# Keeping the split parts of shared weights in DRAM, and a third buffer for the gate operands

## The chip, the core and the metric

The kernel runs on one core of one Trainium2 chip. TensorE multiplies, VectorE, ScalarE (ACT) and GpSimd (POOL) do the elementwise work, SyncE (SP) issues most transfers; ACT and POOL issue some. Each engine runs its own instructions in order. The metric is the device time of one execution in microseconds (us). Three runs of the kernel before gave 3194.96, 3195.38 and 3200.4 us, a median of 3195.38.

## The reference

One encoder block over 1024 tokens with a width of 1024, in float32:

```python
xn = rmsnorm(h, attn_norm_w[l])
proj = xn @ w_in                     # q | k | v | conv B | conv C | conv x | gate a | gate b
y_attn = (rmsnorm(attn, subln_w) * (1 - lambda_init)) @ w_pa     # differential attention
y_conv = (bg * short_conv(cg * xc, conv_w)) @ w_pb
h = h + (sigmoid(ga) * y_attn + sigmoid(gb) * y_conv) @ w_o
hn = rmsnorm(h, ffn_norm_w[l])
sc = einsum('chpd,hpnd->chpn', (hn @ w_query), sub_keys)          # 8 heads x 2 x 128 keys
# 16 best of the pair sums per head -> eidx (of 128*128 experts), g = softmax(top)
out = einsum('chk,chkd->cd', g * gelu(einsum('chkd,cd->chk', expert_u[eidx], hn)), expert_v[eidx])
return rmsnorm(h + out, final_norm_w)
```

## The kernel before

**Two parts of each operand.** TensorE takes a float32 operand here as two parts: a rounded high part `wh` and the rest `wl`, and a product is three matmuls (high by high, high by low, low by high, `THREE` in `gemm`). A weight comes in units of 128 x 2048 numbers, 1.05 MB. `unit` (L207) loads one into a raw tile `wr` on SP, `put` (L183) makes `wh` by a cast on ACT and `wl` by a subtraction on VectorE, or on POOL where `cfg["lo"]` says so. The parts go into a ring of two buffers (`wring`, in some stages a second one, `wloc`). The raw tile has one buffer in most stages, two in the first scores.

**Two groups of tokens.** Group B is the first 640 tokens (`GROUPS`, five tiles of 128), group A the last 384 (three tiles). After q, k and v for all tokens, `mixer` runs for group B: `conv` (six units), `gates` for one gate (four), `gated` (two), attention with the other gate's `gates` between its steps (four), and `gated` again (two). `mix` adds the output projection (four units, `units_k` two at a time). `scores` multiplies by the query weights (eight units) and the keys; group B has two calls, for two tiles and for three. Then group A goes through `mixer`, `mix` and `scores` with the same weights, loaded and split again. So 30 units are used by both groups, and the eight query units three times.

**Selection and gate weights.** `select_gen` (VectorE mostly) takes the 16 best experts per head and token, in two halves per tile; each half ends in two reductions `e`. `weights_gen` (L682) turns the choice of group B's tiles into a dense table of gate weights: per step of four tokens VectorE compares (`ms`, L714), POOL and ACT make the operands `o1` (L718) and `o2` (L720), and one step later `finish` multiplies them on TensorE (`pw`, L695) and copies the product into `wbuf` (L696). Every 32 tokens `wbuf` is stored to `w_d` on ACT's queue (L726). `ms`, `o1` and `o2` have two buffers (`WFB`). These generators are advanced by `tick` along the foreground matmuls, and a scheduler sets the final order on each engine.

**The dense stage.** Afterwards group B's tokens go through all 128 rows of experts: `expert_in` (products `z`, Gelu `pr`, times the gate weights `wt` loaded from `w_d`, L920, split into `ph`) and `expert_out` (products `pout` and `held`). Beside it group A's chosen experts are gathered one by one (`gather_gen`).

**Queues.** SP issues in order: a transfer that waits for its tile holds up those behind it. The gate stores and the scores' stores are on ACT's queue, the gathers and q, k loads on POOL's.

Of the kernel before, what the change touches and what calls it, by code (L numbers as in the profile page):

```python
# [10 lines left out]
F32 = mybir.dt.float32  # L11
# [9 lines left out]
P = 128  # L21
# [30 lines left out]
WQ = 4  # L52
WFB = 2
GATHER = 2.0
# [11 lines left out]
def block_kernel(ctx, tc, x, wqkv, wcols, wpr, wo, wq, skT, uv, uT, an_w, fn_w, fin_w, sub_w,  # L66
# [7 lines left out]
    def pool(name, bufs=1, stack=None, **kw):  # L74
        return (stack or left).enter_context(tc.tile_pool(name=name, bufs=bufs, **kw))
# [10 lines left out]
    dram = pool("dram", space=bass.MemoryType.DRAM)  # L86
# [96 lines left out]
    def put(op, sl, src, lo=V):  # L183
        A.copy(out=op[0][sl], in_=src)  # L184
        lo.tensor_sub(op[1][sl], src, op[0][sl].bitcast(F32))  # L185
# [20 lines left out]

    def unit(wp, src, c):  # L207
        t = cfg["raw"].tile([P, 2048], F32, name="wr", tag="wr")
        SP.dma_start(out=t, in_=src)
        op = operand(wp, [P, 2048], "w")  # L210
        put(op, slice(None), t, cfg["lo"])
        return tuple(t.rearrange("p (k c) -> p k c", c=c) for t in op)

    def units_k(wp, src, n):
        u = [unit(wp, src[n, i], 512) for i in range(2)]
        return [tuple(t[:, k % 4, :] for t in u[k // 4]) for k in range(KD)]
# [244 lines left out]
    def conv(g, n, wring, wloc, xT, uTc):  # L461
        with ExitStack() as st:
            wk = pool("convw", 2, stack=st)
            for ct in range(CT):
                if ct % 2 == 0:
                    wc, wx, wb = (unit(w, wcols[2 * j + ct // 2], 256) for w, j in ((wring, 1), (wring, 2), (wloc, 0)))
                    ys = []
# [34 lines left out]
    def gates(n, wring, xT, j, dst):  # L502
        for dt in range(KD):
            if dt % 2 == 0:
                wg = unit(wring, wcols[6 + 4 * j + dt // 2], 256)
            for c0, cn in halves(n):
                pg = ps['g'].tile([P, cn], F32, name="pg", tag="g")
                gemm(pg, kts(wg, slice((dt % 2) * P, (dt % 2 + 1) * P)), kts(xT, slice(c0, c0 + cn)))
                A.activation(dst[:, dt, c0:c0 + cn], pg, AF.Tanh, scale=0.5)
                yield  # L510

    def gated(n, wring, j, src, g, done):
        for dt in range(KD):
            if dt % 4 == 0:
                wp = unit(wring, wpr[j, dt // 4], 512)
            for c0, cn in halves(n):
                ns = slice(c0, c0 + cn)
                py = ps['g'].tile([P, cn], F32, name="py", tag="g")
                gemm(py, kts(wp, slice((dt % 4) * P, (dt % 4 + 1) * P)), kts(src, ns))
                V.scalar_tensor_tensor(g[:, dt, ns], g[:, dt, ns], 1.0, py, op0=ALU.add, op1=ALU.mult)  # L520
                if done:
                    done((slice(None), dt, ns))

    def mix(tt0, nt, c0, keep_hn, rings, mT, hnT, outer=None):
        with ExitStack() as st:
# [10 lines left out]
            for j in range(2):  # L536
                w = units_k(rings[j], wo, j)
                for i in range(nt):
# [17 lines left out]
    def scores(tt0, nt, c0, rings, hnT, sk, first=None):  # L556
        with ExitStack() as st:
# [14 lines left out]
            for hp in range(2 * PH):  # L572
                if hp % 2 == 0:
                    w = unit(rings[hp // 2 % len(rings)], wq[hp // 2], 256)
                pq = ps["g"].tile([P, n], F32, name="pq2", tag="g")
# [110 lines left out]
    def weights_gen(wf):  # L686
# [11 lines left out]
        for c in range(NB):  # L698
# [9 lines left out]
            for b in range(P // WT):  # L708
                buf = wf.tile([P, NK, WT], F32, name="wbuf", tag="wbuf", bufs=1)
                for q in range(0, WT, WQ):  # L710
# [9 lines left out]
                    A.copy(out=o2.rearrange("p t i -> p i t"), in_=ms[:, 1])  # L720
                    if later:
                        finish(*later.pop(0))
                    later.append((buf, q, o1, o2))
                    yield
                finish(*later.pop(0))
                A.dma_start(out=w_d[c * (P // WT) + b], in_=buf)  # L726
# [132 lines left out]
    wring = pool("wringA", 2, stack=pa)  # L859
    cfg.update(raw=pool("wrawA", 1, stack=pa), lo=V)  # L860
    flat = [t.rearrange("p k t -> p (k t)") for t in operand(act, [P, KD, GB + 2], "actT")]
# [181 lines left out]
```

## Time and profile before

| | |
|---|---|
| median of three runs | 3195.38 us |
| profiled execution | 3191.78 us, span 3190.0 us |
| busy: TensorE, VectorE, ACT, POOL | 3012.1, 2646.3, 1302.9, 923.5 us |
| moved by DMA | 801.11 MB, 251 GB/s on average |
| granted TensorE clock, mean | 0.978 of 2.4 GHz |

Busy time is that of one profiled execution. Matmuls overlap in a pipeline, so a busy TensorE can still have short stalls. A window row gives the busy time of each engine in a stretch, the granted clock, the share of the 16 DMA engines and GB/s. The chain of waits follows the work that ended last back to what released each step. Line numbers are those of the kernel before; in the changed kernel L209 is L216 (raw loads), and its L213 and L222 are the loads and stores of parts.

### The profile page before, as it was taken

Reading aid. Unit: us, or ns where it says so; the run is one execution under the profiler, and the core shown is the slowest. Engines: PE = TensorE matmul, PEld = TensorE weight load, DVE = VectorE, ACT = ScalarE, POOL = GpSimd, SP = SyncE. Lnnn points to the kernel's source line nnn. Section 1 sums busy time; section 2 is a strip of 40 time slices with the busy share of each in tenths; the row PEclk is TensorE's granted clock in tenths of the full one; section 3 lists DMA queues with packets and bytes.
Section 4 is the critical chain, followed back from the end, with each engine's and each line's share of the span. In section 5 each row is a group of like instructions: output and inputs, shape, how many; then the busy total and the mean of one; then the engine's idle time right before and its main releaser. Section 6 shows DMA issues by size and latency. Waiting matters only on the chain.

```text
span 3190.0 us, 45907 instructions
## 1 busy us (share of the span) xinstructions
PE 3012.1 (94%) x17551; PEld 2761.0 (87%) x17551; DVE 2646.3 (83%) x4665; ACT 1302.9 (41%) x2344; POOL 923.5 (29%) x716
## 2 busy tenths in 40 slices
PE   7999999898989879799999999999999999999994
PEld 6799998798988869789989989899889999999993
DVE  5442466378999996799999999999999999999898
ACT  3322364335567766533333333333333333333332
POOL 2310000035344444223222222223332323333333
PEclk9999999999999989899999999999999999999997
DMA  5451232555444375779878888888889999898887
GB/s 180 145 182 67 83 113 80 199 172 213 146 172 157 144 260 196 255 249 333 316 277 321 316 299 309 295 316 293 313 328 343 340 341 348 326 347 325 328 336 281
DMA packets 237549, 801.11 MB, mean 251 GB/s; under 512 B 18832, under 2 KB 123280, under 8 KB 174096
## 3 DMA queue, kind: packets, MB, share of 16 engines
q0 software_dynamic: 64704, 442.53, 37.5%
q1 hardware_dynamic: 152592, 305.30, 27.8%
q10 hardware_dynamic: 20032, 50.34, 4.1%
q8 instruction: 138, 2.26, 0.3%
q14 instruction: 83, 0.68, 0.1%
HBM read 714.74 MB, written 83.36 MB: 250 GB/s over the span
## 4 chain that ended last, share of the span: by engine, by line
PE 56%; DVE 17%; issue 11%; DMA 8%; POOL 4%; ACT 3%; SPq 0%; ACTq 0%; POOLq 0%; DVEq 0%
PE z L905 17%; PE pout L905 10%; PE held L905 6%; PE pq L228 4%; PE pg L228 4%; POOL uvt L739 3%; PE ph L228 3%; DMA uvt<-in_uv,idx 3%; DVE acc L755 2%; PE py L228 2%; PE pw L695 2%; DVE uvt L746 2%; DVE ms L714 1%; PE pv L228 1%; PE pk L228 1%
## 5 line engine op out<-in xcount | busy, mean ns | idle before, releaser
L739 POOL DMA_INDIRECT uvt<-in_uv,idx x384 | 528.1, 1375 | 1288.5 <-DVE acc L755 1011.0
L905 PE MATMUL z<-actTh,uh 128*128 128x320 f32 x2048 | 636.3, 311 | 5.5 <-ACT pr L929 4.5
L905 PE MATMUL z<-actTh,uhl 128*128 128x320 f32 x2048 | 636.5, 311 | 1.1 <-DVE uhl L898 1.1
L905 PE MATMUL z<-actTl,uh 128*128 128x320 f32 x2048 | 635.3, 310 | 0.0
L746 DVE SCALAR_TENSOR_TENSOR uvt<-uvt,hng 128x1024 f32<-128x1024 f32 x384 | 468.0, 1220 | 41.1 <-DMA uvt<-in_uv,idx 40.3
L755 DVE SCALAR_TENSOR_TENSOR acc<-uvt,wt,acc 128x1024 f32<-128x1024 f32 x381 | 487.8, 1280 | 1.3 <-ACT wt L749 1.2
L905 PEld LDWEIGHTS z<-actTh,uh 128*128 128x128 f32 x2048 | 386.0, 188 | 20.5 <-ACT pr L929 8.6
L905 PEld LDWEIGHTS z<-actTl,uh 128*128 128x128 f32 x2048 | 386.2, 189 | 10.1
L905 PEld LDWEIGHTS z<-actTh,uhl 128*128 128x128 f32 x2048 | 386.8, 189 | 8.5 <-DVE uhl L898 2.2
L905 PE MATMUL pout<-vh,ph 128*128 128x512 f32 x768 | 302.5, 394 | 23.2 <-ACT ph L896 15.0
L905 PE MATMUL pout<-vhl,ph 128*128 128x512 f32 x768 | 301.1, 393 | 0.0
L905 PE MATMUL pout<-vh,phl 128*128 128x512 f32 x768 | 300.5, 391 | 0.0
L718 POOL TENSOR_TENSOR o<-ms,wtr 128x512 f32<-128x512 bf16 x160 | 203.0, 1311 | 262.1 <-PE pw L695 123.4
L748 ACT ACTIVATE wt<-zt 128x1 f32<-128x1 f32 x384 | 77.0, 201 | 493.3 <-DVE uvt L746 493.0
L957 DVE TENSOR_TENSOR hacc<-pout,hacc 128x512 f32<-128x512 f32 x384 | 259.4, 681 | 19.6 <-PE pout L905 19.1
L185 DVE TENSOR_TENSOR wl<-wr,wh 128x2048 fp32r<-128x2048 f32 x66 | 157.9, 2392 | 117.7 <-ACT wh L184 117.7
L896 ACT CAST uh<-raw 128x1024 fp32r<-128x1024 f32 x128 | 134.3, 1049 | 193.5 <-DMA raw<-in_uT 187.9
L184 ACT CAST wh<-wr 128x2048 fp32r<-128x2048 f32 x74 | 141.0, 1907 | 168.9 <-DMA wr<-in_wq 31.6
L695 PE MATMUL pw<-o,o 128*128 128x128 f32 x1280 | 169.1, 284 | 41.2 <-POOL o L718 17.6
L695 PEld LDWEIGHTS pw<-o,o 128*128 128x128 f32 x1280 | 161.1, 198 | 49.3 <-issue 25.6
L905 PE MATMUL held<-vhl,ph 128*128 128x512 f32 x512 | 199.6, 391 | 0.0
L720 ACT CAST o<-ms 128x512 f32<-128x512 bf16 x160 | 179.6, 1138 | 38.8 <-DVE ms L714 26.0
(290 smaller groups left out, 6673.5 us busy)
## 6 DMA issues: line engine op xcount, KB each, us to landing
raw<-in_uT SPq DMA_DIRECT2D x128, 512.0 KB
raw<-in_uv SPq DMA_DIRECT2D x128, 512.0 KB
w_d<-wbuf ACTq DMA_DIRECT2D x20, 2048.0 KB
wt<-w_d SPq DMA_DIRECT2D x32, 1280.0 KB
wr<-in_wcols SPq DMA_DIRECT2D x28, 1024.0 KB
wr<-in_wq SPq DMA_DIRECT2D x24, 1024.0 KB
xt<-in_x SPq DMA_DIRECT2D x16, 512.0 KB
q_d<-qt POOLq DMA_DIRECT2D x32, 256.0 KB
```

The lines of the kernel that those rows point to most:

```text
L184: A.copy(out=op[0][sl], in_=src)
L185: lo.tensor_sub(op[1][sl], src, op[0][sl].bitcast(F32))
L228: PE.matmul(pd, lhsT=l[a], rhs=r[b], start=i == 0 and j == 0, stop=i == n - 1 and j == len(c) - 1)
L695: PE.matmul(pw[:, u, :], lhsT=o2[:, t + u, :], rhs=o1[:, t + u, :], start=True, stop=True)
L718: PL.tensor_tensor(out=o1.rearrange("p t i -> p i t"), in0=ms[:, 0], in1=w[:, ts].unsqueeze(1).broadcast_to(sh), op=ALU.mult)
L720: A.copy(out=o2.rearrange("p t i -> p i t"), in_=ms[:, 1])
L739: PL.indirect_dma_start(out=t[:], out_offset=None, in_=uv, in_offset=bass.IndirectOffsetOnAxis(ap=sels[c][1][:, k:k + 1], axis=0))
L746: V.scalar_tensor_tensor(u, u, 1.0, st[c], op0=ALU.mult, op1=ALU.mult, accum_out=zt)
L755: V.scalar_tensor_tensor(st["acc"], v, wt, st["acc"], op0=ALU.mult, op1=ALU.add)
L896: A.copy(out=hi, in_=t)
L905: PE.matmul(ps, lhsT=lhs[k][a], rhs=rhs[k][b], start=first and k == 0 and j == 0, stop=last and k == n - 1 and j == 2)
L957: V.tensor_add(hacc[:, t - NR, ds], ps, hacc[:, t - NR, ds])
```

## The change

At its first use a weight unit with a key is split as before, and the two parts are also stored to DRAM, on SP. At each later use the parts are loaded straight into the ring, without raw tile, cast and subtraction. Group A has no raw tile any more. The gate operands and comparisons get three buffers, and the gate matmuls run two steps after their operands instead of one.

```diff
-WFB = 2
+WFB = 3
...
-    def unit(wp, src, c):
+    parts = {}
+
+    def unit(wp, src, c, key=None):
+        if key in parts:
+            op = operand(wp, [P, 2048], "w")
+            for t, d in zip(op, parts[key]):
+                SP.dma_start(out=t.bitcast(F32), in_=d)
+            return tuple(t.rearrange("p (k c) -> p k c", c=c) for t in op)
         t = cfg["raw"].tile([P, 2048], F32, name="wr", tag="wr")
         SP.dma_start(out=t, in_=src)
         op = operand(wp, [P, 2048], "w")
         put(op, slice(None), t, cfg["lo"])
+        if key:
+            parts[key] = [dram.tile([P, 2048], F32, name="{}{}{}_d".format(*key, hl)) for hl in "hl"]
+            for t, d in zip(op, parts[key]):
+                SP.dma_start(out=d, in_=t.bitcast(F32))
         return tuple(t.rearrange("p (k c) -> p k c", c=c) for t in op)
...
-                wp = unit(wring, wpr[j, dt // 4], 512)
+                wp = unit(wring, wpr[j, dt // 4], 512, ("wp", 2 * j + dt // 4))
...
-                    w = unit(rings[hp // 2 % len(rings)], wq[hp // 2], 256)
+                    w = unit(rings[hp // 2 % len(rings)], wq[hp // 2], 256, ("wq", hp // 2))
...
-                    if later:
+                    if len(later) > 1:
                         finish(*later.pop(0))
                     later.append((buf, q, o1, o2))
                     yield
-                finish(*later.pop(0))
+                while later:
+                    finish(*later.pop(0))
                 A.dma_start(out=w_d[c * (P // WT) + b], in_=buf)
...
-    cfg.update(raw=pool("wrawA", 1, stack=pa), lo=V)
+    cfg.update(raw=None, lo=V)
```

The calls in `conv`, `gates` and `units_k` get keys in the same way as the two shown.

**SP in the first scores.** SP's queue of the kernel before, from the first query weights to the first load of scores for selection (`sc<-sc_d`); `wr` is the raw tile, `hnh_d` and `hnl_d` keep group B's normed rows:

```order
L209 DMA wr<-in_wq 128x2048 x2
L544 DMA h_d<-xt_4713 128x1024
L844 DMA hnh_d<-actTh 1024x1x640
L209 DMA wr<-in_wq 128x2048
L844 DMA hnl_d<-actTl 1024x1x640
L209 DMA wr<-in_wq 128x2048 x5
L603 DMA sc<-sc_d 128x1024
L368 DMA vk<-v_d 128x1024 x2
```

The same place in the changed kernel, where `wq2h_d` is the stored high part of query unit 2 and `wh<-wq0h_d` its reload for the second scores:

```order
L222 DMA wq2h_d<-wh 128x2048
L222 DMA wq2l_d<-wl 128x2048
L216 DMA wr<-in_wq 128x2048
L222 DMA wq3h_d<-wh 128x2048
L222 DMA wq3l_d<-wl 128x2048
L216 DMA wr<-in_wq 128x2048
L222 DMA wq4h_d<-wh 128x2048
L222 DMA wq4l_d<-wl 128x2048
L216 DMA wr<-in_wq 128x2048
L222 DMA wq5h_d<-wh 128x2048
L222 DMA wq5l_d<-wl 128x2048
L216 DMA wr<-in_wq 128x2048
```

Between two raw loads there now stand two stores of the unit split before, and the first reload follows the last raw load.

**ACT at the end of the gate work.** ACT's queue of the kernel before around the last gate store (`w_d<-wbuf`); `uh` and `vh` are the dense stage's first parts, `scs` a tile of scores:

```order
L567 COPY scs<-pcs 128x384
L696 COPY wbuf<-pw 128x128x4 x2
L568 DMA sc_d<-scs 128x3x128
L896 CAST uh<-raw 128x1024
L726 DMA w_d<-wbuf 128x4096
L896 CAST vh<-raw 128x1024 x2
L929 ACT_TABLE_LOAD
L929 ACTIVATE pr<-z 128x640
```

In the changed kernel:

```order
L738 DMA w_d<-wbuf 128x4096
L579 DMA sc_d<-scs 128x3x128
L589 COPY qp<-pq_12033 128x384
L578 COPY scs<-pcs 128x384
L579 DMA sc_d<-scs 128x3x128
L589 COPY qp<-pq_12067 128x384
L578 COPY scs<-pcs 128x384
L579 DMA sc_d<-scs 128x3x128
L656 ACTIVATE tv<-dv 128x64
L589 COPY qp<-pq_12105 128x384
L578 COPY scs<-pcs 128x384
L579 DMA sc_d<-scs 128x3x128
```

The last gate store stood behind the last scores and the first `uh`; now four copies `qp` of score chains follow it, of which these rows show three.

**SP at the start of the dense stage.** SP's queue of the kernel before from the last query weights to the first gate loads (`wt<-w_d`):

```order
L209 DMA wr<-in_wq 128x2048
L913 DMA raw<-in_uT 128x1024
L913 DMA raw<-in_uv 128x1024
L913 DMA raw<-in_uT 128x1024
L913 DMA raw<-in_uv 128x1024
L603 DMA sc<-sc_d 128x1024
L913 DMA raw<-in_uT 128x1024
L913 DMA raw<-in_uv 128x1024
L913 DMA raw<-in_uT 128x1024
L920 DMA wt<-w_d 128x20x128
```

In the changed kernel from the last reload:

```order
L213 DMA wl<-wq7l_d 128x2048
L749 DMA hng<-hn_d 128x1024
L932 DMA wt<-w_d 128x20x128
L925 DMA raw<-in_uT 128x1024
L925 DMA raw<-in_uv 128x1024
L925 DMA raw<-in_uT 128x1024
L932 DMA wt<-w_d 128x20x128
L925 DMA raw<-in_uv 128x1024
```

The first gate load stood behind seven loads of `uT` and `uv`; now it stands ahead of all of them.

## Rows read from the trace of the kernel before

**Rows 1.** windows: stretch, us, busy us of each engine (x instructions), TensorE clock, DMA

```profile
180.00:350.00 170.00, 170.00 (x1154) 169.99 (x1153) 54.01 (x71) 35.05 (x46) 5.88 (x9) 1.00 0.29 104
600.00:680.00 80.00, 66.38 (x473) 63.97 (x472) 43.12 (x119) 32.41 (x48) 11.10 (x5) 0.87 0.77 269
680.00:775.00 95.00, 89.47 (x562) 88.39 (x561) 82.42 (x259) 44.20 (x65) 57.47 (x27) 0.98 0.43 143
775.00:1206.00 431.00, 375.35 (x2385) 352.19 (x2384) 405.07 (x1067) 290.28 (x426) 181.02 (x144) 0.94 0.51 186
1206.00:1312.00 106.00, 104.02 (x710) 103.08 (x708) 73.41 (x171) 69.97 (x101) 44.43 (x34) 1.00 0.47 170
1312.00:1356.00 44.00, 24.94 (x147) 22.69 (x146) 23.60 (x70) 17.37 (x23) 7.54 (x7) 0.81 1.01 353
1356.00:3145.00 1789.00, 1775.43 (x9859) 1608.12 (x9857) 1699.86 (x2533) 615.89 (x1273) 536.16 (x386) 1.00 0.88 318
3145.00:3190.00 45.00, 3.06 (x12) 2.18 (x12) 34.08 (x45) 9.30 (x27) 15.54 (x13) 0.59 0.73 267
```

**Rows 2.** lines of the splits: operands, xcount, busy us, mean ns, idle before

```profile
L185 DVE TENSOR_TENSOR wl<-wr,wh 128x2048 fp32r<-128x2048 f32 x66 | 157.9, 2392 | 117.7 <-ACT wh L184 117.7
...
L184 ACT CAST wh<-wr 128x2048 fp32r<-128x2048 f32 x74 | 141.0, 1907 | 168.9 <-DMA wr<-in_wq 31.6 <-DMA wr<-in_wcols 27.9 <-PE py L228 27.4
...
L185 POOL TENSOR_TENSOR wl<-wr,wh 128x2048 fp32r<-128x2048 f32 x8 | 37.3, 4663 | 78.9 <-ACT wh L184 78.9
```

**Rows 3.** chain of waits: start us, us, what; first scores, group A, dense start

```profile
634.74 2.30 DVE wl L185
...
637.05 4.87 DMA wr<-in_wq
...
791.61 6.19 DMA w_d<-wbuf
...
1317.69 10.34 DMA w_d<-wbuf
...
1328.05 19.98 DMA wt<-w_d
```

**Rows 4.** chain of waits, TensorE: group B's gates; scores of group A

```profile
265.08 56.85 PE pg L228 x384
...
1259.82 4.20 PE pq L228 x24
```

**Rows 5.** windows of 20 us with DMA at a full share

```profile
180.00:200.00 20.00, 20.00 (x140) 19.99 (x139) 6.78 (x10) 4.05 (x6) 5.88 (x9) 1.00 0.97 353
1320.00:1340.00 20.00, 12.38 (x83) 11.86 (x81) 11.21 (x39) 6.26 (x7) 4.82 (x4) 0.92 1.03 387
```

**Rows 6.** lines of VectorE in group A, 775 to 1206 us

```profile
L714 DVE TENSOR_TENSOR ms<-ib,iota_t 128x1024 bf16<-128x1024 bf16 x114 | 89.2, 792 | 8.4 <-ACT o L720 7.3 <-POOL o L718 1.0
L185 DVE TENSOR_TENSOR wl<-wr,wh 128x2048 fp32r<-128x2048 f32 x23 | 58.3, 2536 | 6.5 <-ACT wh L184 6.5
...
L640 DVE TENSOR_REDUCE e<-sc 128x64 f32<-128x1024 bf16 x12 | 25.0, 2088 | 0.0
...
L591 DVE MAX8 sv<-tk 128x8 f32<-128x128 f32 x56 | 16.1, 288 | 0.9
```

**Rows 7.** waits in group A: engine line <- releaser: us, times, longest

```profile
POOL o L718 <- DVE ms L714: 86.2, 33, 12.8
...
PE pw L695 <- ACT o L720: 12.6, 10, 4.2
PE pw L695 <- POOL o L718: 11.7, 10, 2.0
PE pw L695 <- ACT wbuf L696: 10.9, 3, 9.2
```

**Rows 8.** timeline of TensorE, dense start: start us, us, instruction, idle before

```profile
1334.40 0.31 PE L905 MATMUL z<-actTh,uhl 128*128 128x320 f32 x1
1349.75 0.79 PE L905 MATMUL pout<-vh,ph 128*128 128x512 f32 x1 [15.03 <-ACT ph L896]
```

More of the change, by code (lines that the diff above doesn't have):

```diff
@@ L211, in unit, with units_k @@
         put(op, slice(None), t, cfg["lo"])
+        if key:
+            parts[key] = [dram.tile([P, 2048], F32, name="{}{}{}_d".format(*key, hl)) for hl in "hl"]
+            for t, d in zip(op, parts[key]):
+                SP.dma_start(out=d, in_=t.bitcast(F32))
         return tuple(t.rearrange("p (k c) -> p k c", c=c) for t in op)
-    def units_k(wp, src, n):
-        u = [unit(wp, src[n, i], 512) for i in range(2)]
+    def units_k(wp, src, n, key=None):
+        u = [unit(wp, src[n, i], 512, key and (key, 2 * n + i)) for i in range(2)]
         return [tuple(t[:, k % 4, :] for t in u[k // 4]) for k in range(KD)]
@@ L465, in conv @@
                 if ct % 2 == 0:
-                    wc, wx, wb = (unit(w, wcols[2 * j + ct // 2], 256) for w, j in ((wring, 1), (wring, 2), (wloc, 0)))
+                    wc, wx, wb = (unit(w, wcols[2 * j + ct // 2], 256, ("wc", 2 * j + ct // 2)) for w, j in ((wring, 1), (wring, 2), (wloc, 0)))
                     ys = []
@@ L504, in gates @@
             if dt % 2 == 0:
-                wg = unit(wring, wcols[6 + 4 * j + dt // 2], 256)
+                wg = unit(wring, wcols[6 + 4 * j + dt // 2], 256, ("wc", 6 + 4 * j + dt // 2))
             for c0, cn in halves(n):
@@ L536, in mix @@
             for j in range(2):
-                w = units_k(rings[j], wo, j)
+                w = units_k(rings[j], wo, j, "wo")
                 for i in range(nt):
```

## The prediction

> **What bounds the kernel now.** I read the windows by stage first, then the lines of the weight splits, then the chain of waits where a stage begins. [rows 1] cut the span by stage. From 1356 to 3145 us TensorE is busy 1775 of 1789 us; nothing in that stage is changed, so I look ahead of it. Group B's projections (180 to 350) are TensorE alone, with DMA at a share of 0.29. The first scores (600 to 680) are different: DMA share 0.77, TensorE 66 of 80 us, granted clock 0.87, so part of it at 1.2 GHz instead of 2.4. Group A (775 to 1206) has VectorE busy 405 of 431 us (94%) and TensorE 375, and there the splits of weights stand among the selection and the gate work. Group A's scores (1206 to 1312) are TensorE again, 104 of 106. From 1312 to 1356 TensorE is busy 25 of 44 us: the dense stage starts and waits.
>
> **What is removed and added, in counts.** A split is an ACT cast (1.91 us), and a VectorE (2.39 us) or POOL (4.66 us) subtraction; there are 74 [rows 2]. Of these 30 stay as first uses and 6 are the q, k, v weights, so 38 go: the 8 POOL ones and 30 of 66 on VectorE. Each first use adds two stores of 1.05 MB on SP, 60 in all; each later use loads 2.1 MB in place of 1.05 MB. DMA moves about 63 MB more in stores and 40 MB more in loads, all before 1312 us. What was a load, a cast and a subtraction ahead of TensorE becomes a load alone, but one that cannot start before TensorE has left the slot, where the raw tile could be fetched early.
>
> **Group B, 180 to 600: +9 us.** The raw tile has one buffer, so units follow in a chain: load 4.87 us, cast 1.91, subtraction 2.30 make 9.1 us [rows 2, 3]. TensorE uses a unit for 14.2 us: 56.85 for four [rows 4]. So the chain has 5.1 us to spare. After the change SP issues the two stores of a unit ahead of the next load. They wait for the cast and the subtraction, and behind them on SP stand that load, in attention the `vk` loads too; the load lands behind their bytes: 2.1 MB at 353 GB/s, the rate at a share of 0.97 [rows 5], is 5.9 us, so a link becomes 15.0 us, 0.8 more than a unit lasts. Over the twelve units of conv, gates and the first projection that is 10 us, less the 5 spared at the start. The fourth output unit of the mix, used 12 matmuls after the third, comes 6 us later, of which I count 4. Sum +9. Below, the stores are hidden wholly: 0. Above, a store of 2.1 MB lasts as long as the slower of the two writes of that size, 10.34 us against 6.19 [rows 3]: a link of 19.4, 12 x 5.2 - 5 = +57. I take the rate, since DMA is otherwise at 0.29 there.
> The Trainium skill (DMA: Bandwidth & Descriptors, section Anatomy of one DMA) gives 2.0 us fixed plus the bytes at 436 GB/s, for DMAs issued by GpSimd; by it the three transfers, overlapped, take an estimated 9.2 us, the link 13.4, and this term would be 0. Its 4.4 us for a load of 1.05 MB stands against the 4.87 of the trace, so I keep the trace's rate.
>
> **Scores of group B, 600 to 775: +12 us.** The first scores moved 269 GB/s x 80 us = 21.5 MB [rows 1]. The stores of the first six query units come into the same stretch: 12.6 MB. 34.1 MB at 353 GB/s are 97 us: +17. At 387 GB/s, the highest rate at a full share [rows 5], it is +8; at the stretch's own 269, +47. The order puts the selection's first load behind the last raw load and the reload of unit 0, so selection starts later too. The second scores then go through one raw buffer: load 4.87, cast 1.91, POOL 4.66 are 11.4 us a unit, 92 of the 95 us; this chain goes. But TensorE is busy 89.5 of 95 [rows 1], so I take back 5. Their DMA, 13.6 MB plus 4.2 of stores and 8.4 of longer loads, needs 74 us at 353 GB/s and is not the limit. Range 0 to +42.
> By the Trainium skill (HBM Reference, section Specifications (TRN2)) a core streaming alone gets about 425 GB/s; by that the 34.1 MB would take an estimated 80 us and the first scores would lose nothing. The trace at a full share shows 387.
>
> **Group A, 775 to 1206: -22 us.** VectorE loses 23 subtractions of 2.54 us = 58 [rows 6]. The built order puts work in their place: between conv A's first product and the last hn split stand 114 `ms` comparisons instead of 106 (8 x 0.79 = 6 us) and seven half tiles of selection instead of six. A half costs about 21 us, an estimate from [rows 6]: 8 x 5 search instructions near 0.28, half as many again on the candidates, two reductions of 2.09. Net -31, 33 us of time at 94%. ACT's 23 casts are off the path (290 of 431 us busy). Against it: two buffers a ring, so the reload for unit u+2 starts when u ends and is due when u+1 ends, 8.4 us later (two times 4.20 [rows 4]) and a little for gate work. It takes 5.9 us and a landing latency of about 1.9 (4.87 less its bytes at 353 GB/s), so it is hidden when alone, and late beside a 2.1 MB gate write. About 22 units with half a microsecond each: +11. Net -22.
> TensorE waits 12.6 and 11.7 us for the gate operands [rows 7]. Three buffers, used two steps on, could give all 24 back, or nothing: POOL itself waits 86 us for VectorE's `ms` in this stage, so the operand is late since VectorE is, and I count it inside VectorE's 31. Wait on PSUM copies (10.9) stays. Range of the stage: -50 (everything) to +10 (reloads late at every unit, 22 x 1.5, and the relief filled).
>
> **Group A's scores: 0.** Eight splits go, but TensorE is at 98%. A unit lasts 106/8 = 13 us, so a reload of 7.8 us is covered; without that cover it costs 8 x 3.
>
> **Start of the dense stage: -15 us.** In [rows 3] the last gate write is issued at 1317.69, lands in 10.34, then the gate load takes 19.98 among raw loads and gathers, then come `pr`, `ph`, and only then `pout`: TensorE stands still 15.03 us [rows 8]. After, the last gate matmul stands four score chains (4 x 4.2 = 17 us) before the first `z`, the write ends inside the scores, and SP issues the gate load ahead of the raw tiles. The stall goes; next is the raw `uT`, 1.3 MB further behind in SP's queue, +3 to +4, against it TensorE's 4 us at half clock after the stall, which should go too. So -15, with -19 and 0 as ends, the latter if gathers slow the gate load as before.
>
> **Dense stage and tail: 0.** No instruction of it changes; one half tile of selection more or less is covered by TensorE. The last gathers end 45 us after TensorE [rows 1], and their order against the dense work is the same.
>
> **Sum.** 9 + 12 - 22 + 0 - 15 = -16. The profiled execution took 3191.78 us (span 3190.0), so 3176; the median of the runs is 3.6 above it: 3179.
>
> **Rivals.** (1) DMA hides everything and VectorE's relief is kept: 0 + 3 - 35 - 19 = -51, 3144. For it: DMA shares of 0.29 and 0.51 in groups B and A. Against: 0.77 in the first scores. (2) Reloads on two buffers eat group A's gain: 9 + 12 - 4 - 15 = +2, 3197. For it: each reload waits for TensorE; against: TensorE has 56 us to spare in that stage. (3) Slower: SP's queue in group B. A store is issued when its split is done, and the next raw load behind it; as soon as two stores take more than 5.1 us, TensorE waits for every unit from conv to the first projection, and if they take 8.5 us, the middle between 6.19 and 10.34 with an issue, 12 x 3.4 - 5 + 4 = +40 there, +20 in the first scores, -10 in group A (its loads suffer the same), -15 at the start: +35, 3230. For it: 5.9 is already over 5.1; against: DMA is idle for 0.7 of that stretch. (4) The gate edit does nothing, being a wait on VectorE: inside the forecast.
>
> **How the numbers follow.** Forecast 0.50 (its own range 3163 to 3195), rival 1 0.16, rival 2 0.14, rival 3 0.20. The range 3140 to 3218 holds the first three nearly whole and some of the last. 0.2% is 6.4 us, about what a measurement tells from no change. Faster: 0.43 + 0.16 + 0.02 = 0.61; within: 0.05 + 0.09 = 0.14; slower 0.25.
>
> **What would show it.** VectorE's subtraction of `wl` 36 times; in 180 to 350 TensorE still full or with gaps before `px`, `pg`; the first scores longer and DMA share near 1; group A shorter than 431 us with VectorE still over 90%; no 15 us gap between `z` and the first `pout`. I am wrong if group A is no shorter, or if group B grows by tens of microseconds.

## The result, and the profile after

The changed kernel takes 3239.39 us (median of 4 runs, 3233.61 to 3242.66); before, measured beside it, takes 3195.17. The ratio is 1.0139, 95% interval 1.0113 to 1.0165: slower by about 44 us. The forecast was 3179, with 3218 as the upper end of its range.

Three lines of the profile page of the changed kernel: the span, the busy time of each engine, and the bytes moved.

```profile
span 3237.2 us, 46003 instructions
...
PE 3027.4 (94%) x17551; PEld 2774.6 (86%) x17551; DVE 2576.4 (80%) x4635; ACT 1234.7 (38%) x2306; POOL 884.7 (27%) x708
...
HBM read 754.59 MB, written 146.28 MB: 278 GB/s over the span
```

The change did what it says: 146.28 MB written in place of 83.36, VectorE 2576 us busy in place of 2646. One line of the page counts the splits that are left, 36 of 66 on VectorE [rows 2]:

```profile
L185 DVE TENSOR_TENSOR wl<-wr,wh 128x2048 fp32r<-128x2048 f32 x36 | 82.4, 2289 | 133.5 <-ACT wh L184 127.6
```

The windows by stage of the changed kernel, which answer to [rows 1]. They begin and end at the same matmuls as the rows there (the first at the end of q, k and v), so the stages answer to each other; gate matmuls that a run does in another stage move with it. Columns: stretch, its length, busy us of PE, PEld, DVE, ACT, POOL with their instructions, granted clock, DMA share, GB/s.

```profile
180.80:358.60 177.80, 174.30 (x1161) 174.03 (x1162) 56.23 (x72) 37.38 (x49) 7.07 (x10) 0.98 0.64 242
606.70:707.20 100.50, 71.65 (x489) 67.94 (x488) 34.13 (x67) 30.73 (x49) 1.67 (x3) 0.81 1.00 391
707.20:789.00 81.80, 80.00 (x496) 79.33 (x496) 55.21 (x225) 20.63 (x44) 15.21 (x11) 1.00 0.71 269
789.00:1239.00 450.00, 386.62 (x2453) 363.98 (x2451) 398.12 (x1155) 260.24 (x424) 193.71 (x159) 0.94 0.59 223
1239.00:1354.30 115.30, 111.81 (x736) 110.70 (x734) 52.42 (x145) 62.62 (x97) 38.43 (x33) 0.96 0.72 274
1354.30:1391.00 36.70, 23.39 (x122) 21.37 (x122) 16.02 (x21) 12.39 (x20) 7.84 (x7) 0.81 0.99 357
1391.00:3190.80 1799.80, 1777.57 (x9852) 1609.06 (x9851) 1704.28 (x2581) 617.42 (x1269) 543.64 (x383) 1.00 0.87 316
3190.80:3237.20 46.40, 3.03 (x12) 2.17 (x12) 34.23 (x45) 9.39 (x28) 14.94 (x13) 0.59 0.70 259
```

Group B is the first row: TensorE now has gaps. The first scores (second row) run 100 us with DMA full. Group A (fourth row) is 450 us long where it was 431; VectorE fell from 94% of it to 88%, and TensorE's idle part rose from 56 to 63 us. The last-but-one row is the dense stage, 11 us longer.

Of the 58 us of subtractions that left VectorE in group A, its busy time shows only 7 (405 to 398 us, in a stage 19 us longer). Two lines show what came instead:

```profile
L725 DVE TENSOR_TENSOR ms<-ib,iota_t 128x1024 bf16<-128x1024 bf16 x125 | 106.2, 861 | 11.6 <-POOL o L729 7.4 <-ACT o L731 4.2
L651 DVE TENSOR_REDUCE e<-sc 128x64 f32<-128x1024 bf16 x16 | 33.5, 2094 | 0.1
```

Against [rows 6] these are 125 comparisons in place of 114, each 861 ns long in place of 792, and 16 reductions (eight half tiles of selection) in place of 12; the forecast had counted on seven half tiles.

The timeline of TensorE at the start of the dense stage, which answers to [rows 8]: the 15 us ahead of the first `pout` are gone, and 11.74 us now stand ahead of the first `z`.

```profile
1366.11 0.63 PE L917 MATMUL z<-actTh,uh 128*128 128x320 f32 x1 [11.74 <-ACT uh L908]
...
1384.60 0.31 PE L917 MATMUL z<-actTh,uhl 128*128 128x320 f32 x1
1384.75 0.40 PE L917 MATMUL pout<-vh,ph 128*128 128x512 f32 x1
```

The table gives the stages in us, each as one profiled execution minus that of before (3190.0). They are measured between the same matmuls in every run: the last output product of group B's mix, the first and the last query product of the second scores and of group A's scores, and the first `pout`. Beside the changed kernel stand the runs with one edit alone and the one without the subtractions (all told below); the control shows what such a difference is worth where nothing that matters was changed.

| stage | forecast | changed | parts alone | gate edit alone | no subtractions | control |
|---|---|---|---|---|---|---|
| to the end of group B's mix | +9 | +6.7 | +4.4 | -1.4 | +1.6 | +2.1 |
| first scores | +17 | +20.5 | +19.4 | -0.1 | +0.6 | +0.1 |
| second scores | -5 | -13.1 | -14.5 | +11.2 | +7.1 | +1.0 |
| group A | -22 | +18.9 | -2.3 | +15.4 | -17.8 | -7.8 |
| group A's scores | 0 | +9.4 | +16.1 | +10.7 | +4.7 | 0.0 |
| from there to the first `pout` | -15 | -7.3 | +0.6 | -7.3 | +8.6 | -0.7 |
| dense stage and tail | 0 | +12.1 | +11.6 | +3.9 | -4.3 | +4.9 |
| sum | -16 | +47.2 | +35.3 | +32.4 | +0.6 | -0.3 |

The gate work and the selection are spread over the four middle rows, and what one of them does less the next does more; so they are best read together: forecast -42, changed +7.9, parts alone -0.1, gate edit alone +30.0, no subtractions +2.6, control -7.5.

All of these kernels run the same 17551 matmuls of the same shapes. With the median distance from one start to the next that each shape has in the kernel before, they need 2936 us. What differs is the rest: stalls (distances of more than 2.3 times that median) of 154 us before and 190 after, and 50 and 59 us of shorter delays. So 36 of the 47 us are stalls of TensorE.

### The profile page after: what moved, and what is told of

It is laid out like the page before. It is cut to its first block, busy times and chain, and to the rows that moved or that the text cites. A ratio compares the mean times of both kernels' runs of the same rounds, so it can differ in the third digit from the quotient of the medians.

```text
span 3237.2 us, 46003 instructions
## 1 busy us (share of the span) xinstructions
PE 3027.4 (94%) x17551; PEld 2774.6 (86%) x17551; DVE 2576.4 (80%) x4635; ACT 1234.7 (38%) x2306; POOL 884.7 (27%) x708
## 3 DMA queue, kind: packets, MB, share of 16 engines
HBM read 754.59 MB, written 146.28 MB: 278 GB/s over the span
## 4 chain that ended last, share of the span: by engine, by line
PE 31%; DVE 25%; issue 9%; DMA 8%; POOL 3%; ACT 1%; POOLq 0%; DVEq 0%; SPq 0%; ACTq 0%
PE z L917 12%; PE pout L917 6%; DMA uvt<-in_uv,idx 5%; DVE acc L767 5%; PE held L917 4%; DVE uvt L758 4%; PE pw L706 2%; DVE hacc L969 2%; PE pq L239 2%; POOL uvt L751 2%; DMA raw<-in_uT 2%; DVE vhl L910 2%; DVE uhl L910 2%; DVE ms L725 1%; PE ph L239 1%
## 5 line engine op out<-in xcount | busy, mean ns | idle before, releaser
L751 POOL DMA_INDIRECT uvt<-in_uv,idx x384 | 536.5, 1397 | 1272.6 <-DVE acc L767 900.1
L917 PE MATMUL z<-actTh,uh 128*128 128x320 f32 x2048 | 638.3, 312 | 20.5 <-ACT uh L908 11.7
L758 DVE SCALAR_TENSOR_TENSOR uvt<-uvt,hng 128x1024 f32<-128x1024 f32 x384 | 476.2, 1241 | 46.6 <-DMA uvt<-in_uv,idx 46.3
L917 PEld LDWEIGHTS z<-actTh,uhl 128*128 128x128 f32 x2048 | 388.4, 190 | 11.7 <-DVE uhl L910 5.4
L729 POOL TENSOR_TENSOR o<-ms,wtr 128x512 f32<-128x512 bf16 x160 | 193.5, 1255 | 232.4 <-PE pw L706 137.3
L941 ACT ACTIVATE pr<-z 128x640 f32<-128x640 f32 x128 | 90.0, 703 | 259.6 <-PE z L917 237.0
L185 DVE TENSOR_TENSOR wl<-wr,wh 128x2048 fp32r<-128x2048 f32 x36 | 82.4, 2289 | 133.5 <-ACT wh L184 127.6
```

The lines of the kernel that those rows point to most:

```text
L729: PL.tensor_tensor(out=o1.rearrange("p t i -> p i t"), in0=ms[:, 0], in1=w[:, ts].unsqueeze(1).broadcast_to(sh), op=ALU.mult)
L751: PL.indirect_dma_start(out=t[:], out_offset=None, in_=uv, in_offset=bass.IndirectOffsetOnAxis(ap=sels[c][1][:, k:k + 1], axis=0))
L758: V.scalar_tensor_tensor(u, u, 1.0, st[c], op0=ALU.mult, op1=ALU.mult, accum_out=zt)
L917: PE.matmul(ps, lhsT=lhs[k][a], rhs=rhs[k][b], start=first and k == 0 and j == 0, stop=last and k == n - 1 and j == 2)
L941: A.activation(p.rearrange("p (h c) -> p h c", h=len(hs)), z, AF.Gelu)
```

## The experiments

Two theories stood against each other at first. By the first, the parts make the loss: their stores fill DMA (called the traffic theory below), their reloads come late behind other transfers on SP (queue theory), or they come late since their slot in the ring comes free late (buffer theory). By the second, the gate edit makes it (gate theory).

**The gate edit alone.** Here `ms` keeps two buffers, where the changed kernel has three, and group A's mix has one row buffer less.

```
-WFB = 2
+WFB = 3
...
-                    if later:
+                    if len(later) > 1:
                         finish(*later.pop(0))
...
-                finish(*later.pop(0))
+                while later:
+                    finish(*later.pop(0))
```

> Only the gate edit, on the kernel before: o1 and o2 in three buffers and used two steps on (ms stays at two buffers and group A's mix has one row buffer less, so that it fits). If the loss comes from the parts, by whatever way (queue, buffers or traffic theory): within 10 us of before, 3185 to 3205, group A 405 to 435 us long. If the gate edit itself makes the loss by moving selection and gate work against each other (gate theory): 3215 or more, group A 20 us or more longer.

3224.78 us, ratio 1.0095 (1.0066 to 1.0125). The time is that of the gate theory, though the edit only gives TensorE's operands more time; group A grew by 15 us over before, not by 20. From the first query product of the second scores to the last one of group A's, TensorE is idle 57.5 us in the control below and 87.7 here, and these 30 us are as much as the run loses. Ahead of `pw` it is idle less, 30.1 us in place of 37.0. It is idle more ahead of the key products `pcs`, which wait for ACT's copies `qp` (9.8 in place of 0.2), ahead of the `hn` transposes (11.2 in place of 2.8), ahead of the transposes `ptw` that open a block of gate work and wait for VectorE's last reduction `e` (10.5 in place of 3.0), and ahead of the attention scores `ps` (12.6 in place of 6.7).

**The parts alone.** The changed kernel with `WFB = 2` and the old order of use.

> Only the stores and reloads; gate operands in two buffers, used one step on, as before. Queue, buffer and traffic theories: the loss stays, 3230 to 3250, group A from first product of conv to last output product 415 to 430 us against 388 before. Gate theory: most of it goes, 3200 to 3218.

3226.08 us, ratio 1.0089 (1.0060 to 1.0118). Below the 3230 named for the first theory and above the 3218 of the second: both were incomplete. Each edit costs some 30 us alone, and together they cost 44, not 60. One reason that the costs do not add up: with the parts the gate work begins later (the first `pw` at 784 us in the changed kernel, at 754 in the run of the gate edit, at 737 in the control), and the changed kernel has no wait ahead of `ptw` at all.

**No stores.**

```
+            if parts:
+                parts[key] = list(parts.values())[0]
+            else:
                 parts[key] = [dram.tile(...) for hl in "hl"]
                 for t, d in zip(op, parts[key]):
                     SP.dma_start(out=d, in_=t.bitcast(F32))
```

> The changed kernel, but only the first unit's parts are stored; every later use loads those, so 58 of 60 stores of 1.05 MB are gone while all reloads, and their place, stay (the later weights are therefore the wrong ones). Traffic theory (stores fill DMA): 3190 to 3205. Queue and buffer theories: only group B (+9) and the first scores (+19, of which -12 came back) are won back, 3218 to 3230, and group A stays 30 us or more longer than before.

3212.12 us, ratio 1.0053 (1.0033 to 1.0072): 27 us back, of which the first scores give 17. This is below the 3218 of the queue and buffer theories and above the 3205 of the traffic theory. The stores are more than half of the loss, and that half comes back with all reloads in place.

**Score loads on POOL.** In the changed kernel SP issues the load of the selection's scores, and stands still until VectorE has freed the score tile. The row of this wait in group A before, and the first two rows of SP's waits there in the changed kernel (engine, line waited at, releaser: us, times, longest):

```profile
SPq L603 <- DVE e L640: 83.8, 6, 36.0
```
```profile
SPq L614 <- DVE e L651: 135.4, 6, 40.1
SPq L213 <- PE pg L239: 69.5, 6, 18.2
```

```
-            SP.dma_start(out=sc, in_=sc_d[...])
+            PL.dma_start(out=sc, in_=sc_d[...])
```

> The changed kernel with the selection's score loads issued by POOL in place of SP: they wait for VectorE there, and no reload stands behind them. Queue theory: group A gets 25 to 40 us back, 3200 to 3215, and TensorE no longer waits for reloads of the projections in group A. Buffer and traffic theories: within 8 us of the changed kernel, 3231 to 3247.

3222.14 us, ratio 1.0086 (1.0057 to 1.0114): 17 us less than the changed kernel, between the ranges of the queue theory (3200 to 3215) and of the others (3231 to 3247). They come from group A, from its second projection above all. Its windows before, in the changed kernel, and in this run:

```profile
1085.30:1127.30 42.00, 37.44 (x264) 35.57 (x263) 41.39 (x126) 32.47 (x52) 18.85 (x17) 1.00 0.52 194
```
```profile
1106.30:1171.70 65.40, 50.19 (x322) 48.49 (x322) 55.66 (x161) 37.62 (x64) 27.42 (x21) 0.84 0.41 161
```
```profile
1108.40:1153.40 45.00, 37.10 (x246) 35.92 (x245) 43.49 (x105) 27.16 (x47) 21.58 (x19) 0.89 0.65 236
```

TensorE's idle time in that stage is 4.6, 15.2 and 7.9 us; in the changed kernel 58 matmuls more fall in it too (322 in place of 264), and the granted clock is 0.84 in place of 1.00. But the way there is not the one that I had expected. In group A of the changed kernel no matmul waits for a reload. The chain of waits of the changed kernel shows the way (start us, us, what):

```profile
1114.35 2.03 DVE e L651
1116.39 8.90 DMA sc<-sc_d
1125.31 1.07 DVE sv L599 x5
1126.38 0.60 DVE ms L725
1127.00 1.09 ACT o L731
1128.09 0.33 ACT ga L520
1128.46 1.11 PE pt L191 x4
```

VectorE frees the score tile with `e`; the load is issued at once and lands in 8.90 us; VectorE stands in order at the search `sv` until then. Behind the search is the comparison `ms`; ACT's `o` waits for that, the gate activation `ga` stands behind `o` on ACT, and TensorE's transposes wait 9.2 us for `ga`, which frees their PSUM tile. Four engines in a row wait for one load of 0.5 MB. VectorE is idle at the head of this chain, not busy. The load itself was issued as soon as the tile came free, so SP did not hold it up; but the two reloads that SP had held up behind it were issued 1.0 and 1.7 us later, and while the load ran DMA was at a share of 0.92. This chain accounts for 9 of the 17 us; where the others come from was not followed. A slow load alone does not cost this: one at 1005 us of this run took 9.48 us, and one at 828 us of the kernel before 10.20.

**A control.** The kernel before, with the row buffer less that the gate edit alone and some later runs needed in group A's mix to fit.

> The kernel before with one row buffer less in group A's mix, the side change that the run of the gate edit alone carried. If that run's +30 us came from the gate edit: within 6 us of before, 3189 to 3202, and the dense stage (first pout to last z) 1770 to 1780 us as before. If it came from the side change, or if any new order of the work costs that much: 3210 or more, the dense stage near 1787.

3195.62 us, ratio 1.0002 (0.9990 to 1.0015). The side change costs nothing that can be measured, and the +30 us is the gate edit's. Its profile also shows the spread of a stage from one execution to another: -7.8 in group A, +4.9 in the dense stage and tail.

**Stores on POOL.** `PL.dma_start(out=d, ...)` in place of SP.

> The changed kernel with the 60 stores of parts issued by POOL, so that the next raw load no longer stands behind them on SP; the bytes are the same. Queue theory: group B's +9 and most of the first scores' +19 go, 3212 to 3225. Traffic theory: the first scores keep 12 us or more of the +19, 3230 to 3242.

3237.89 us, ratio 1.0136 (1.0116 to 1.0155), as the changed kernel. The first scores without stores, and with them on POOL (the changed kernel's are in the second row of the windows above):

```profile
603.50:684.00 80.50, 63.93 (x462) 61.23 (x460) 39.73 (x111) 28.01 (x43) 1.68 (x3) 0.87 0.86 319
```
```profile
606.20:711.00 104.80, 69.15 (x470) 65.42 (x468) 32.19 (x64) 29.20 (x46) 10.14 (x19) 0.80 0.99 379
```

With the stores DMA is full on either queue, and the stage is 24 us longer than without. There it is bytes, not the order on SP. In group B's conv the gaps went (163.5 of 163.5 us busy from 186.5 to 350): conv takes 86.4 us from its first product to the first of the gates, 91.7 in the changed kernel and 86.3 before. But the stretch from the end of the first projection to the first output product is 3 us longer than in the changed kernel; to the end of the mix 5 of the 7 us are left.

**No parts of the query weights.** `unit(..., wq[hp // 2], 256)` without a key.

> The changed kernel without parts of the query weights: the scores load, cast and subtract them each time as before (a raw tile of their own in group A's scores); all other parts are stored and reloaded. The first scores should lose their +19 and the second their -12; the sum of the other terms stays: 3228 to 3238. If the query stores also disturb what follows (selection starts later): 3210 to 3225.

3230.18 us, ratio 1.0107 (1.0090 to 1.0124), within the expected 3228 to 3238. The first scores took 74.8 us, 3.7 less than before, and the second ones 104.0, 10 more. Against the changed kernel that is 24 us less in the first scores and 23 more in the second, so what the reload gives in the second is about what its stores cost in the first; some of either number is gate work that moved.

**Score loads on POOL in the kernel before.** The edit of the fourth run, alone.

> The kernel before, with the selection's score loads issued by POOL in place of SP, nothing else. If the wait of these loads on SP costs only where reloads replaced early raw loads: within 6 us of before, 3189 to 3201. If it costs in both kernels: 3175 to 3187, and this is the faster version.

3186.89 us, ratio 0.9980 (0.9969 to 0.9992): faster than the kernel before by 0.2%, with an interval that just leaves out no change, and at the upper end of the range expected if both kernels pay for this wait. Its profiled execution took 3194.2, 7 us over the median, so no stage is read from it.

**Three buffers, used one step on.** `WFB = 3` on the control, with `ms` kept at two buffers.

> The kernel before (with the control's side change), o1 and o2 in three buffers, but still used one step on. If the third buffer makes the loss (the comparisons ms and POOL's products run ahead and push other work back on VectorE): 3212 to 3228 as the gate edit. If the use two steps on makes it: within 6 us of before, 3189 to 3201.

3216.59 us against 3199.26 on this chip, ratio 1.0059 (1.0042 to 1.0076): the buffer alone costs about 19 us. Between the first query product of the second scores and the last of group A's, TensorE is idle 77.2 us, 20 more than in the control, as much as the run costs: 15.5 of it stand ahead of `ptw`, which waits 18.5 us for VectorE's `e` in place of 3.0, and 7.9 ahead of `pcs`, which waits for ACT's `qp`; the gaps ahead of `pw` are 5 us shorter. The stretch from the last query product of the second scores to conv A's first product shows how the order changed, in the control and here:

```profile
776.80:790.90 14.10, 10.21 (x70) 9.55 (x68) 12.83 (x49) 11.51 (x16) 7.30 (x8) 0.88 1.01 379
```
```profile
780.80:810.60 29.80, 14.97 (x78) 13.99 (x77) 23.07 (x56) 16.00 (x21) 13.13 (x12) 0.71 0.74 281
```

By the same windows for `pw` alone, 64 gate matmuls stand ahead of conv's first product in place of 56. In the control 16 of them stand among the last score products; here all 64 come behind those, one after the other, with nothing between them to work on while the next operand is made, and conv begins 15.7 us later in its stage. The transposes `ptw` stand earlier in TensorE's queue than the selection delivers. The waits of this kind in the second scores alone, in the control and here:

```profile
PE ptw L703 <- DVE e L640: 1.9, 2, 1.3
```
```profile
PE ptw L703 <- DVE e L640: 6.5, 1, 6.5
```

**The lag carried over a block's end.** The gate edit, with the waiting operands kept when a block of 32 tokens ends and the gate store behind the block's last use (`if q + WQ == WT: A.dma_start(out=w_d[blk], in_=buf)`).

> The gate edit alone, but the two waiting operands are carried over a block's end (32 tokens) in place of being used up there together, and the gate store follows the block's last use. If the loss of the gate edit is the bunching at block ends (two uses, a store and a new block in one step): most of its 30 us go, 3190 to 3205. If it is the third buffer or the later use itself: 3215 to 3230.

3231.97 us, ratio 1.0099 (1.0081 to 1.0117), no less than the gate edit. Bunching at a block's end is not the cause.

**Stores without reloads, twice.** The first of these kernels was meant to store 60 parts, but stored at every use, 136 in all; the expectation below is for another kernel than the one that ran.

```
-        if key in parts:
+        if key in parts and False:
```

> The run with the parts alone, but nothing is reloaded: 60 stores, then raw load, cast and subtraction for every use as before. Its cost over before is that of the stores: if only group B and the first scores pay, +20 to +26, 3214 to 3221, with group A as long as before. If the reloads bring a gain in group A that something else hides, this run is slower than the run with the parts alone (3226): 3235 or more.

3366.00 us, ratio 1.0524 (1.0506 to 1.0542). It shows only that 76 more stores, most of them in group A, are ruinous. With the condition mended (`if key and key not in parts:` ahead of the stores):

> The run with the parts alone, but only the 60 first-use stores, none of the reloads (the run before that was meant so stored at every use, 136 stores). If the stores make the loss of the parts: 3214 to 3226, as the parts alone. If half of it is the reloads': 3204 to 3213.

3250.06 us, ratio 1.0174 (1.0144 to 1.0205): +52 us, outside both ranges. Without reloads the stores cost 0.85% or 27 us more than with them. The second scores, with these stores and the old way of splitting, and with reloads (the run with the parts alone):

```profile
697.90:817.10 119.20, 98.06 (x569) 94.66 (x568) 107.48 (x345) 48.68 (x70) 60.83 (x28) 0.89 0.42 146
```
```profile
703.30:782.90 79.60, 79.38 (x472) 78.99 (x472) 42.38 (x157) 17.32 (x37) 10.73 (x7) 0.97 0.69 259
```

So in this stage the run without reloads takes 40 us more than the one with them, part of it for 97 matmuls more, gate work that the other does later; and 25 us more than the kernel before, which has about as many matmuls there (562 and 569). TensorE waits 8.4 us for ACT's `qp` and 9.8 for the parts `wh` and `wl` in it. Why the old way of splitting loses so much here, after the stores, is not shown.

**The parts in their cheapest form.** No query parts, gate operands as before, score loads on POOL.

> Parts alone in their cheapest form: no parts of the query weights, gate operands as before, score loads on POOL. Against the kernel before with score loads on POOL (3187): if VectorE's relief of 15 subtractions in group A is worth time, the +7 of group B is paid back and it comes to 3165 to 3185; if TensorE's waits there do not depend on VectorE's load, 3192 to 3210.

3212.63 us, ratio 1.0050 (1.0033 to 1.0067), outside even the range for "no gain from VectorE" by 3 us. Against the kernel before with the same score loads (ratio 0.9980) it is some 0.7% slower, with 22 subtractions fewer on VectorE (44 of 66 are left; the 15 above was a miscount).

**No subtractions in group A.** This decides the forecast's main term. Group A's units are cast only, and the cast stands in for the low part; nothing else differs from the kernel before.

```
+        if cfg.get("one"):
+            hi = wp.tile([P, 2048], F32R, name="wh", tag="wh")
+            A.copy(out=hi, in_=t)
+            op = (hi, hi)
...
+    cfg.update(raw=pool("wrawA", 1, stack=pa), lo=V, one=True)
```

> The kernel before, where group A's units (22 in its projections, 8 in its scores) are cast only and the cast stands in for the low part too: 30 VectorE subtractions gone, no DMA, queue or buffer changed, TensorE's matmuls the same in number and shape (the low part's products are wrong numbers). If VectorE's share of 94% bounds group A, as the forecast had it (net 31 to 35 us): 3158 to 3168. If TensorE's waits there do not depend on VectorE's load: 3188 to 3202. If a new order of the work alone costs: 3205 or more.

3193.35 us against 3197.78, ratio 0.9991 (0.9975 to 1.0008): no difference. Group A's windows and two kinds of its waits, in the control:

```profile
776.80:1201.20 424.40, 375.30 (x2396) 353.47 (x2394) 402.37 (x1067) 289.17 (x427) 183.80 (x145) 0.95 0.52 189
```
```profile
POOL o L718 <- PE pw L695: 100.9, 28, 9.7
POOL o L718 <- DVE ms L714: 78.4, 33, 12.8
...
PE pw L695 <- POOL o L718: 14.0, 9, 3.3
PE pw L695 <- ACT wbuf L696: 11.3, 3, 9.4
...
PE pw L695 <- ACT o L720: 6.7, 10, 2.7
```

and without the subtractions:

```profile
782.90:1197.30 414.40, 368.55 (x2330) 348.66 (x2329) 356.55 (x1060) 278.39 (x416) 169.87 (x141) 0.94 0.51 187
```
```profile
POOL o L723 <- PE pw L700: 112.3, 32, 13.3
POOL o L723 <- DVE ms L719: 52.3, 23, 12.9
...
PE pw L700 <- ACT o L725: 13.1, 10, 5.5
...
PE pw L700 <- POOL o L723: 10.2, 3, 4.6
```

VectorE's busy time falls from 402 to 357 us and POOL waits 26 us less for `ms`. TensorE is idle 49 us in the control and 46 here. The stage is 10 us shorter with 7 us less of TensorE's work in it, and the stages around it are longer by more. From the first query product of the second scores to the last of group A's, TensorE is idle 58.5 us here and 57.5 in the control: its waits did not change. Behind that the start of the dense stage is 9 us longer than in the control, where a `pw` waits 10.3 us for ACT's copy `wbuf`, and the dense stage 9 us shorter; neither is part of the forecast's term for group A.

**Two that settled nothing new.** Score loads on POOL with the third buffer (`PL.dma_start` in the run of three buffers), and a quicker pace of the selection in the changed kernel (`SEL_STEP = 1.4`, score loads on POOL).

> The run with the third operand buffer alone, with the selection's score loads on POOL. If that buffer costs because these loads come late on SP (VectorE waited 16 us for them in the second scores, 8 in the control): 3185 to 3200. If its cost is elsewhere: 3208 to 3222.

3218.99 us, ratio 1.0067 (1.0037 to 1.0098). The third buffer's loss is not the late score load. (VectorE waited 14.3 us for these loads in the run of three buffers, up to conv A's first product; the 16 us of the expectation are those of the gate edit alone.)

> The changed kernel with score loads on POOL and the selection paced at 1.4 in place of 1.5, so that one more half tile is searched ahead of the dense stage. If the dense stage's +11 is the 9 us of searches that VectorE took over there: dense stage 1776 to 1784, and 3208 to 3216 in all against 3222. If not: dense stage 1786 or more.

3220.21 us, ratio 1.0091 (1.0059 to 1.0123), the dense stage 1790 us up to its last `z`. It didn't test what it should: the selection was no further on at the start of the dense stage than in the run with the score loads on POOL (40 searches `si` of scores were left in both).

## Why the prediction was wrong

**Group B, +9.** Right in sign and near in size: +6.7. The size is luck. The chain of 15.0 us a unit was to hold TensorE up in all twelve units, but the gates and the first projection take 84.8 us after and 84.9 before. The loss is 3.3 us ahead of conv's first product and 5.4 in conv, and 2 of them come back by the end of the mix. That SP's order is the way held for conv: with the stores on POOL its 5.4 us go, and most of the stage's loss stays.

**First scores, +17.** Right in the mechanism: +20.5, from the stores' bytes at a full DMA. Its size is two errors that nearly cancel: 39.3 MB were moved, not 34.1, since the stores of all eight units and the first reloads fell into the stage, and they were moved at 391 GB/s, not at 353. The Trainium skill (HBM Reference, section Specifications (TRN2)) puts a core alone at about 425 GB/s, by which the 39.3 MB would take an estimated 92 us. The trace moved 391 on average, 435 in single slices of 2.5 us, and took 100. **Second scores, -5**: mis-sized, -13.1, of which 7 us are gate matmuls moved on to later stages.

**Group A, -22: the step that failed.** It took the 58 us of subtractions that VectorE loses in a stage where it was 94% busy, filled part of the room with other work, and turned the rest into time. The run without the subtractions shows that the whole 58 us, with no reload to pay, is worth nothing that can be measured (a ratio of 0.9991, and 0.9975 at the lower end is 8 us). VectorE was busy because the selection, which group A doesn't need, is put into its queue at a pace set by TensorE's work; it was not what TensorE waited for. In the changed kernel the room was filled with more of the same: its busy time fell by 7 us, not by 31. The evidence was in the waits of before. I read POOL's 86.2 us for `ms` [rows 7] as proof that VectorE is late, and left out the row ahead of it, from the same answer:

```profile
POOL o L718 <- PE pw L695: 89.7, 25, 10.4
```

POOL waited as long for TensorE to free its operand as for VectorE to deliver the comparison. I read this as a ring of engines that wait for one another in order, whose length is set by the order and the latencies rather than by one engine's load; that it is the order is argued here, not shown.

**The gate edit, "all 24 back, or nothing".** Failed too, and on the other side: alone it costs about 30 us, most of it with the third buffer, and on top of the parts 13. The forecast had given it a gain or nothing and no possible loss. Where a third buffer costs is shown: the built order opens a block of gate work before the selection is ready (15.5 us), puts key products ahead of their copies (7.9) and gate matmuls in a heap ahead of conv. A late score load, and bunching at a block's end, were tried and are not it. Why the order comes out so stays open.

**Reloads, +11 in group A.** The forecast's mechanism, a reload that is late since its slot frees late, didn't show: no wait of TensorE in group A names a reload in the changed kernel, and 2.7 us do in the run of the parts alone. What cost there was the score load on SP with the reloads behind it, and VectorE's order behind the load: 17 us. It needs both edits: with the parts alone the same loads are on SP, and group A is 2.3 us shorter than before.

**Start of the dense stage, -15.** The mechanism was right, the gate load no longer stands on the path. The size was off, -7.3, since the raw `uT`, which I had priced at +3 to +4, now holds TensorE for 11.7 us: ACT's cast `uh` waits 10.0 us for it. The time at half clock did not go either: it moved from the first `pout` (4 us) to the first `z`, which run at 0.47 us each in place of 0.31 for 6 us (granted clock 0.51 from 1359 to 1373 us).

**Group A's scores and the dense stage, 0.** +9.4 and +12.1. Some of the first is gate work that arrives later. In the second, VectorE makes 40 of the `si` searches of scores in the dense stage in place of 32; but the run with the parts alone has 32 and is 11.6 us longer all the same. With 5 us between two executions that do the same, this part stays open.

**The rivals.** The slower one came near the size (3230) by luck: group B's queue was to give +40 of it and gave 7. The second had group A's gain eaten, but by late reloads, which did not show. The fourth let the gate edit do nothing, and it cost. The loss is from several places: the stores in the first scores, group A with the score load, group A's scores, and the dense stage; none of them alone is large.

## What to carry to other kernels

That an engine is 94% busy does not show that it bounds a stage. Read both directions of each wait, take off the filler work that the stage doesn't need, and where it matters run the kernel without the work in question. In a kernel of in-order queues with an order worked out beforehand, another buffer or a later use is an edit of that order on every engine, and its price in a forecast needs a bound for a loss as well as for a gain. A load that waits for a tile to come free belongs on a queue where nothing urgent stands behind it: here this alone made the kernel before 0.2% faster.

## What was not expected of the hardware

Stores and loads together moved 391 GB/s over 100 us at a DMA share of 1.00 with the stores on SP, and 379 at 0.99 with them on POOL, so the queue made little difference. Slices of 2.5 us within the first reached 435, and other stretches at a full share moved 353 and 387 [rows 5]: a full share stands for no single rate. A load of 0.5 MB took 4.1 us (the median of four from 650 to 800 us of the control), 8.90 us behind VectorE's `e` in the changed kernel, where two reloads followed it onto a DMA at a share of 0.92, and 10.20 at 828 us of the kernel before; its size alone does not say which.
